# A DRAM to DRAM copy as the first DMA of the ScalarE queue in a pooling kernel

## The chip, the cores and the metric

The kernel runs on one core of a Trainium2 chip. The core has engines that run beside each other: VectorE (DVE), ScalarE (ACT), GpSimd (POOL), SyncE (SP) and TensorE, which has no work here. Data moves between DRAM and the on-chip memory SBUF by 16 DMA engines. A DMA is issued by an instruction on SyncE's or ScalarE's queue; the engine that issued it goes on, and whoever needs the data waits for a semaphore. PSUM is a second, smaller on-chip memory. The metric is device time in microseconds (us) of one execution; lower is better.

## The reference

The input x is 32 x 256 x 4096 float32 (134.2 MB), the output 32 x 256 x 1024 (33.6 MB). Each output is the 2-norm mean over four neighbours:

```python
    for i in range(out_length):
        start = i * kernel_size
        end = start + kernel_size
        window = np.abs(x[:, :, start:end]) ** p
        result[:, :, i] = (np.mean(window, axis=-1)) ** (1.0 / p)
```

with p = 2 and kernel_size = 4, so out = sqrt((a² + b² + c² + d²) / 4).

## The kernel before

All of x is one flat array that is cut into six blocks; each block is laid out as 128 rows, one for each SBUF partition. Blocks 0 to 3 and 4 are cut further into tiles of up to W = 13184 columns: 20 tiles in all, one with 13152 columns (tile 3) and a shorter last one (11680). A tile of W columns is 6592 KB.

Three SBUF buffers `xt` (`X_SLOTS`, tile i in buffer i modulo 3) hold the tiles. `load(i)` (L83) issues tile i's load on SyncE. Its 128 rows are 52,736 bytes each. Three loads are issued at the start (L122-123); load i + 3 is issued when tile i is summed and its buffer is free (L144-145).

For every tile, ScalarE squares it in place (`square`, L89), VectorE adds the two halves of each group of four (`pairs`, L95) and then the two sums that are left (`fours`, L99), and ScalarE takes the root with the factor 1/4 (`root`, L102). The sums of four tiles side by side make one output block in the buffer `ot`; the sum of the first tile of the next block goes to a PSUM buffer `st`, so that it does not wait for the store of `ot`.

There are six stores (`store`, L86). Stores 0, 1 and 2 are issued on ScalarE's queue (L116, called from `roots` for the groups that end in tiles 3, 7 and 11), stores 3, 4 and 5 on SyncE's queue (L147, L168, L172). `rows(flat, b, div)` (L64) gives block b of a flat array as 128 rows; `rows(of, 0, k)` is the part of the output that store 0 writes, 128 rows of 13176 floats, and `rows(xf, 0, 1)` the input of block 0, 128 rows of 52704 floats.

The order of instructions is written out by hand (`manual_schedule`, L62). On ScalarE the first instructions are the load of the function table and a root of one constant column (`first`, L129), which has the table loaded before data arrives. Then follow the squares in tile order, with roots between them. Waits between instructions are put in by the framework from what each one reads and writes; `implied` takes out some that others cover. DMAs take their semaphores from eight, in turn; a DMA that reuses a semaphore waits until the DMA that had it before has landed.

Of the kernel before, what the change touches and what calls it, by code (L numbers as in the profile page):

```python
# [1 line left out]

# [4 lines left out]


@with_exitstack
def kernel(  # L10
    ctx: ExitStack,
    tc: tile.TileContext,
    x: bass.AP,
    p: float,
    kernel_size: int,
    out: bass.AP,
):

    nc = tc.nc

    assert float(p) == 2.0, "kernel specialized for p == 2"
    k = int(kernel_size)  # L30
    assert k == 4, "kernel specialized for kernel_size == 4"

    P = nc.NUM_PARTITIONS
    fp32 = mybir.dt.float32
    Act = mybir.ActivationFunctionType
    add = mybir.AluOpType.add
    xf = x.rearrange("b c l -> (b c l)")
    of = out.rearrange("b c l -> (b c l)")
    total = xf.shape[0] // P

    W = 13184
    R = W // k
    X_SLOTS = 3
    NARROW = W - 32
    LAST = total - 18 * W - NARROW
    widths = [W] * 3 + [NARROW] + [W] * 15 + [LAST]
    n = len(widths)
    assert 0 < LAST <= W and LAST % 16 == 0


    blocks = [[0, 1, 2, 3], [4, 5, 6, 7], [8, 9, 10, 11], [12, 13, 14, 15], [18, 16, 17], [19]]
    block_of = {i: b for b, group in enumerate(blocks) for i in group}
    block_width = [sum(widths[i] for i in group) for group in blocks]

    x_pool = ctx.enter_context(tc.tile_pool(name="x_pool", bufs=1))
    o_pool = ctx.enter_context(tc.tile_pool(name="o_pool", bufs=1))
    s_pool = ctx.enter_context(tc.tile_pool(name="s_pool", bufs=1, space=bass.MemoryType.PSUM))
    x_tiles = [x_pool.tile([P, W], fp32, name=f"xt{j}") for j in range(X_SLOTS)]
    o_tile = o_pool.tile([P, 4 * R], fp32, name="ot")
    first = o_pool.tile([P, 1], fp32, name="first")  # L60
    s_tile = s_pool.tile([P, 4096], fp32, name="st")
    ctx.enter_context(tc.manual_schedule())  # L62

    def rows(flat, b, div):  # L64
        at = sum(block_width[:b]) * P // div
        return flat[at:at + block_width[b] * P // div].rearrange("(p w) -> p w", p=P)


    free = x_tiles[17 % X_SLOTS]
    place = {i: o_tile[:, i % 4 * R:i % 4 * R + widths[i] // k] for i in range(16)}  # L70
    place[18] = free[:, R:2 * R]
    place[19] = free[:, 0:LAST // k]
    place[16] = free[:, 2 * R:3 * R]
    place[17] = free[:, 3 * R:4 * R]
    held = [o_tile[:, 0:w // k] for w in block_width[:4]] + [free[:, R:4 * R], place[19]]

    xs, loads, stores, sums, squares = {}, {}, {}, {}, {}

    def load(i):
        b = block_of[i]  # L80
        at = sum(widths[j] for j in blocks[b][:blocks[b].index(i)])
        xs[i] = x_tiles[i % X_SLOTS][:, 0:widths[i]]
        loads[i] = nc.sync.dma_start(out=xs[i], in_=rows(xf, b, 1)[:, at:at + widths[i]])  # L83

    def store(b, queue):
        stores[b] = queue.dma_start(out=rows(of, b, k), in_=held[b])  # L86

    def square(v):
        return nc.scalar.activation(out=v, in_=v, func=Act.Square)  # L89

    def pairs(v):

        q = v.rearrange("p (n j) -> p n j", j=k)
        h = v[:, 0:v.shape[1] // 2].rearrange("p (n j) -> p n j", j=2)
        return nc.vector.tensor_tensor(out=h, in0=q[:, :, 0:2], in1=q[:, :, 2:4], op=add)  # L95

    def fours(o, v):
        h = v[:, 0:v.shape[1] // 2].rearrange("p (n j) -> p n j", j=2)
        return nc.vector.tensor_tensor(out=o, in0=h[:, :, 0], in1=h[:, :, 1], op=add)  # L99

    def root(o, s):
        return nc.scalar.activation(out=o, in_=s, func=Act.Sqrt, scale=1.0 / k)  # L102

    summed = {i: s_tile[:, 0:R] if i in (4, 8, 12, 16) else place[i] for i in range(n)}

    def roots(*group):
        if len(group) == 1:
            root(place[group[0]], summed[group[0]])
        else:
            v = o_tile[:, group[0] % 4 * R:(group[-1] % 4 + 1) * R]  # L110
            r = root(v, v)
            if group[0] in (5, 9):

                implied(r, stores[block_of[group[0]] - 1])
        if group[-1] in (3, 7, 11):
            store(block_of[group[-1]], nc.scalar)  # L116

    def implied(later, earlier):

        tc.declare_no_dep(later.ins, earlier.ins, reason="implied by the other waits")  # L120

    for i in range(X_SLOTS):  # L122
        load(i)


    ahead = {4: (3,), 8: (7,), 12: (11,)}
    behind = {3: [(0, 1, 2)], 7: [(5, 6), (4,)], 11: [(9, 10), (8,)], 14: [(12,)], 15: [(13, 14)], 16: [(15,)]}

    root(first[:, :], nc.const_aps.tensor(1.0, (P, 1), fp32))  # L129
    for i in range(17):  # L130
        if i in ahead:
            roots(*ahead[i])
        s = square(xs[i])
        squares[i] = s
        if i == 3:
            implied(s, squares[0])
        if i in (3, 7, 11):

            for earlier in sums[i - X_SLOTS]:
                implied(s, earlier)  # L140
        for group in behind.get(i, []):
            roots(*group)
        sums[i] = pairs(xs[i]), fours(summed[i], xs[i])
        if i + X_SLOTS < n:  # L144
            load(i + X_SLOTS)

    store(3, nc.sync)  # L147
    square(xs[17])
    pairs(xs[17])
    fours(summed[17], xs[17])  # L150
    later = {18: 4608, 19: 2000}

    def shared_square(i):
        v = xs[i][:, 0:later[i]]
        nc.vector.tensor_tensor(out=v, in0=v, in1=v, op=mybir.AluOpType.mult)  # L155
        square(xs[i][:, later[i]:widths[i]])

    def shared_pairs(i):
        implied(pairs(xs[i]), loads[i])

    shared_square(18)
    roots(16)
    roots(17)
    shared_pairs(18)
    fours(summed[18], xs[18])
    shared_square(19)
    roots(18)
    store(4, nc.sync)  # L168
    shared_pairs(19)
    fours(summed[19], xs[19])  # L170
    roots(19)
    store(5, nc.sync)  # L172


# [1 line left out]
_INS = ['x', 'p', 'kernel_size']  # L176
_OUTS = [((32, 256, 1024), 'float32')]

_NUMBERS = {'p': 2.0, 'kernel_size': 4}


# [26 lines left out]
```

## Time and profile before

| | |
|---|---|
| median of 3 runs | 393.97 us (393.89 to 394.08) |
| span of the profiled execution | 392.3 us (its only time on the page; 1.7 us under the median) |
| VectorE busy | 218.2 us, 56%, 42 instructions |
| ScalarE busy | 274.4 us, 70%, 37 instructions |
| HBM read, written | 134.22 MB, 33.55 MB, together 428 GB/s over the span |
| chain that ended last | DMA 43%, ACT 30%, DVE 23% |
| a square of a full tile (L89) | 11.19 us |
| `pairs`, `fours` of a full tile (L95, L99) | 7.03, 3.59 us |

The span runs from the first to the last instruction of the profiled execution; the timed runs include what lies around it. In the slices of the page a digit is the busy share in tenths. "To landing" is the time from the issue of a DMA to its last byte's arrival. A group in the profile names the line, the engine, the operation and the tiles; "ACTq" and "SPq" are DMA issues on those queues, which are not counted as busy time. Bracketed at the end of a timeline's line is how long the engine was idle before, and what ended that.

### The profile page before, as it was taken

The page shows a single profiled execution, that of the slowest core. Times are in us where ns is not written, and L with a number is a line of the kernel's source. Part 1 is how long each engine was busy: PE and PEld are TensorE (multiplying, and loading weights), DVE is VectorE, ACT ScalarE, POOL GpSimd, SP SyncE. Part 2 cuts the span into 40 slices and gives each one's busy share as a digit, 9 for nine tenths or more (in the row PEclk, how much of TensorE's full clock was granted, in tenths as well). Part 3 has the DMA queues.
Part 4 walks back from the last instruction along what each step waited for, and adds up shares of the span by engine and source line. Part 5 has one row for each costly group of instructions (what it writes and reads, how often), then busy time and mean ns, then how long its engine had stood idle before and what let it go on. Part 6 is the DMA issues. An engine that isn't in the chain of part 4 may idle for free.

```text
span 392.3 us, 176 instructions
## 1 busy us (share of the span) xinstructions
DVE 218.2 (56%) x42; ACT 274.4 (70%) x37; POOL 0.2 (0%) x4
## 2 busy tenths in 40 slices
DVE  0009477580693274905942748069418485699970
ACT  1095695979950859799509597995098999969910
POOL 0000000000000000000000000000000000000000
DMA  8999999999999999999999999999999999999997
GB/s 344 430 430 430 430 440 435 452 457 366 430 430 430 430 430 430 430 441 446 452 446 441 436 430 436 430 430 430 430 430 430 430 430 430 430 453 415 430 413 342
DMA packets 3744, 167.77 MB, mean 428 GB/s; under 512 B 416, under 2 KB 416, under 8 KB 416
## 3 DMA queue, kind: packets, MB, share of 16 engines
q1 hardware_dynamic: 3312, 147.53, 87.4%
q10 hardware_dynamic: 432, 20.25, 11.9%
HBM read 134.22 MB, written 33.55 MB: 428 GB/s over the span
## 4 chain that ended last, share of the span: by engine, by line
DMA 43%; ACT 30%; DVE 23%; issue 0%; ACTq 0%; SPq 0%; DVEq 0%
DMA xt<-in_x_dram 43%; ACT xt L89 28%; DVE xt L95 14%; DVE ot L99 5%; DVE xt L99 3%; DVE xt L155 2%; ACT ot L102 2%; ACT xt L102 1%; ACTq L86 0%; SPq L83 0%; DVEq L95 0%
## 5 line engine op out<-in xcount | busy, mean ns | idle before, releaser
L89 ACT ACTIVATE xt<-xt 128x13184 f32<-128x13184 f32 (+3 forms) x20 | 216.7, 10847 | 92.3 <-DMA xt<-in_x_dram 91.0
L95 DVE TENSOR_TENSOR xt<-xt 128x6592 f32<-128x6592 f32 (+2 forms) x20 | 139.7, 6985 | 144.1 <-ACT xt L89 143.9
L99 DVE TENSOR_TENSOR ot<-xt 128x3296 f32<-128x3296 f32 (+1 forms) x13 | 46.7, 3592 | 17.9 <-DMA out_dram<-ot 17.6
L102 ACT ACTIVATE ot<-ot 128x6592 f32<-128x6592 f32 (+3 forms) x8 | 37.2, 4655 | 7.0 <-DVE ot L99 7.0
L102 ACT ACTIVATE xt<-xt 128x3296 f32<-128x3296 f32 (+1 forms) x3 | 8.5, 2836 | 8.8 <-DVE xt L99 8.8
L99 DVE TENSOR_TENSOR st<-xt 128x3296 f32<-128x3296 f32 x4 | 14.4, 3600 | 0.1
L99 DVE TENSOR_TENSOR xt<-xt 128x3296 f32<-128x3296 f32 (+1 forms) x3 | 10.4, 3461 | 0.1
L102 ACT ACTIVATE ot<-st 128x3296 f32<-128x3296 f32 x3 | 8.7, 2898 | 0.0
L155 DVE TENSOR_TENSOR xt<-xt 128x4608 f32<-128x4608 f32 (+1 forms) x2 | 7.2, 3593 | 0.0
L102 ACT ACTIVATE xt<-st 128x3296 f32<-128x3296 f32 x1 | 2.9, 2898 | 0.0
L102 ACT ACT_TABLE_LOAD x1 | 1.3, 1283 | 0.7 <-PEq L189 0.7
L102 ACT ACTIVATE first<-const-float32-1.0 128x1 f32<-128x1 f32 x1 | 0.2, 202 | 0.0
L189 POOL MEMSET const-bfloat16-1.0<- 128x1 bf16 x1 | 0.1, 101 | 0.0
L189 POOL MEMSET const-uint8-127<- 128x1 uint8 x1 | 0.1, 101 | 0.0
L189 POOL MEMSET const-float32-0.0<- 128x1 f32 x1 | 0.1, 98 | 0.2 <-issue 0.2
L189 POOL MEMSET const-float32-1.0<- 128x1 f32 x1 | 0.1, 98 | 0.0
## 6 DMA issues: line engine op xcount, KB each, us to landing
xt<-in_x_dram SPq DMA_DIRECT2D x18, 6592.0 KB, 29.8
out_dram<-ot ACTq DMA_DIRECT2D x2, 6592.0 KB, 35.1
out_dram<-ot SPq DMA_DIRECT2D x1, 6592.0 KB, 37.1
out_dram<-ot ACTq DMA_DIRECT2D x1, 6588.0 KB, 36.3
xt<-in_x_dram SPq DMA_DIRECT2D x1, 6576.0 KB, 24.7
xt<-in_x_dram SPq DMA_DIRECT2D x1, 5840.0 KB, 21.9
out_dram<-xt SPq DMA_DIRECT2D x1, 4944.0 KB, 16.1
out_dram<-xt SPq DMA_DIRECT2D x1, 1460.0 KB, 8.2
```

The lines of the kernel that those rows point to most:

```text
L89: return nc.scalar.activation(out=v, in_=v, func=Act.Square)
L95: return nc.vector.tensor_tensor(out=h, in0=q[:, :, 0:2], in1=q[:, :, 2:4], op=add)
L99: return nc.vector.tensor_tensor(out=o, in0=h[:, :, 0], in1=h[:, :, 1], op=add)
L102: return nc.scalar.activation(out=o, in_=s, func=Act.Sqrt, scale=1.0 / k)
L155: nc.vector.tensor_tensor(out=v, in0=v, in1=v, op=mybir.AluOpType.mult)
L189: nc = _bacc.Bacc("TRN2", target_bir_lowering=False, num_devices=1)
```

## The change

After the three first loads have been issued, and ahead of ScalarE's first instruction, ScalarE's queue gets one DMA from DRAM to DRAM. It reads every eighth of the 128 rows of block 0 of x, 2048 floats of each, and writes them to every eighth of the 128 rows that store 0 writes later: 16 rows of 8192 bytes, 131,072 bytes in all. Store 0 overwrites all of them with the result. No other instruction is changed or moved in its queue.

```diff
     for i in range(X_SLOTS):
         load(i)
+    BULK = 2048
+    nc.scalar.dma_start(out=rows(of, 0, k)[0:P:8, 0:BULK], in_=rows(xf, 0, 1)[0:P:8, 0:BULK])
 
 
     ahead = {4: (3,), 8: (7,), 12: (11,)}
```

Since the copy and store 0 write the same bytes, store 0 waits for the copy. The copy takes the first of the eight DMA semaphores, so that the semaphore of every later DMA moves by one; load 6 is now the first to reuse one, the copy's.

## The prediction

> **What bounds the kernel now.** I read the page first, for the DMA row over the 40 slices and for the queues.
>
> ```profile
> DMA  8999999999999999999999999999999999999997
> GB/s 344 430 430 430 430 440 435 452 457 366 430 430 430 430 430 430 430 441 446 452 446 441 436 430 436 430 430 430 430 430 430 430 430 430 430 453 415 430 413 342
> ...
> q1 hardware_dynamic: 3312, 147.53, 87.4%
> q10 hardware_dynamic: 432, 20.25, 11.9%
> ```
>
> The DMA engines are full from the second slice to the last but one, while DVE has 56% and ACT 70% of the span. q1 carries what SyncE issues, q10 what ScalarE issues: the three first stores, 20.25 MB. One slice away from the two ends is low: the tenth, 88 to 98 us, with 366 GB/s at a full DMA row.
>
> Second view, the timeline of ScalarE; each square starts 0.02 us after its load has landed if ScalarE was waiting.
>
> ```profile
> 0.73 1.28 ACT L102 ACT_TABLE_LOAD   x1 [0.73 <-PEq L189]
> 0.73 338.28 SPq L83 DMA_DIRECT2D xt<-in_x_dram  x20
> ...
> 18.79 11.19 ACT L89 ACTIVATE xt<-xt 128x13184 f32<-128x13184 f32 x1 [16.56 <-DMA xt<-in_x_dram]
> ...
> 34.35 11.19 ACT L89 ACTIVATE xt<-xt 128x13184 f32<-128x13184 f32 x1 [4.38 <-DMA xt<-in_x_dram]
> ...
> 65.47 11.16 ACT L89 ACTIVATE xt<-xt 128x13152 f32<-128x13152 f32 x1 [4.34 <-DMA xt<-in_x_dram]
> ...
> 90.31 0.38 ACTq L86 DMA_DIRECT2D out_dram<-ot  x1
> 90.73 22.27 ACT L89 ACTIVATE xt<-xt 128x13184 f32<-128x13184 f32 x2 [0.46 <-ACT ot L102]
> ...
> 128.86 11.19 ACT L89 ACTIVATE xt<-xt 128x13184 f32<-128x13184 f32 x1 [15.86 <-DMA xt<-in_x_dram]
> ```
>
> One load of 6.75 MB takes 34.35 - 18.79 = 15.56 us, 434 GB/s, at full stream. Load 0 was issued at 0.73 and landed at 18.77, 18.04 us later: 2.48 us more than its bytes take, the price of starting from an empty stream.
>
> Third view, windows laid between such landings. Each of the three holds four transfers of the same bytes, three loads and one store of ScalarE's queue (loads 4 to 6 and store 0; loads 8 to 10 and store 1; loads 12 to 14 and store 2). The columns are the window, its length, the busy time of DVE, ACT and POOL with their counts, the clock, the DMA share and GB/s.
>
> ```profile
> 65.47:128.86 63.39, 36.70 (x8) 44.71 (x6) 0.00 (x0) 1.00 1.00 426
> 144.41:206.65 62.24, 36.67 (x8) 44.80 (x7) 0.00 (x0) 1.00 1.00 434
> 222.22:284.49 62.27, 36.81 (x8) 44.80 (x6) 0.00 (x0) 1.00 1.00 434
> ...
> 92.00:96.00 4.00, 0.00 (x0) 4.00 (x1) 0.00 (x0) 1.00 1.12 395
> 96.00:100.00 4.00, 0.00 (x0) 4.00 (x1) 0.00 (x0) 1.00 0.97 422
> ...
> 171.00:175.00 4.00, 0.00 (x0) 4.00 (x1) 0.00 (x0) 1.00 1.03 448
> ```
>
> The first stretch is 63.39 - 62.26 = 1.13 us longer for the same work. The four-microsecond windows place the loss: 92 to 96 us, 1.7 us after store 0 was issued, has 395 GB/s at a share of 1.12; the same place behind store 1 (171 to 175) has 448. In the packet records of the trace every one of the 16 engines has one row of a *load* that starts at 91.9 to 92.4 us and takes 2.6 to 3.1 us; the usual row takes 1.947. The first rows of store 0 start only behind these. So **the first DMA of ScalarE's queue makes all 16 engines stand still for about 1 us; the second and third do not.** SyncE's first store, at 339.10, shows no such loss, though it is the first store of its queue. The first rows of load 0 took 2.0 to 3.0 us too.
>
> Is the end still bound by DMA, so that a microsecond gained at 92 us arrives there? Store 3 was issued at 339.10 and landed 37.1 us later, at 376.2. Store 4, issued at 371.76, landed 16.1 us later, at 387.9; its 5.06 MB at 434 GB/s are 11.7 us: it began where store 3 ended. Store 5 landed at 391.4, 3.5 us after store 4, and its 1.495 MB are 3.45 us. The stream does not run dry up to the last byte.
>
> **The change part by part.** Nothing is removed. Added is one DMA issue on ScalarE, ahead of its table load, of 16 rows of 8192 bytes, and waits that follow from it.
>
> (1) *Issue on ScalarE.* The nearest row is the first ACTq issue, 0.38 us. Table load and first root (1.28 + 0.20) move from 0.73 to about 1.11. Cover: the 16.56 us that ScalarE idles before 18.79. Cost 0; without that cover, 0.38. SyncE's first loads are on another queue and are not moved.
>
> (2) *Waits.* Store 0 now waits for the copy also (both write the first store's rows), and load 6 does (the copy has taken one of the eight DMA semaphores, so each DMA's number moves by one and load 6 reuses the copy's). Both come at 87 to 90 us, over 80 us after the copy; neither waits. A second wait costs a semaphore instruction; three on L86 of SyncE took 17 ns each. On ScalarE that delays square 4, DVE's sums, and so load 7, which comes at 112.6 and has until load 6 has landed at 128.84: 16 us of cover, cost 0. Later pairs on one semaphore are as far apart as before.
>
> (3) *Bytes of the copy.* 131,072 B at 434 GB/s are 0.30 us on 16 engines, 8192 B each. Ahead of the span the trace has 8 KB packets of 0.31 to 0.55 us, one engine each. Lower bound 0: the copy goes in the 2.48 us before load 0 runs at full rate. Upper bound, beside the opening below, 0.55. I take **+0.30**: all three first loads are queued, so every engine that copies delays load rows.
>
> (4) *The opening of ScalarE's queue* moves from 92 us to 1 to 3 us. At 92 us this takes away **-1.13**. At the start it costs between 0 (it passes beside SyncE's own opening, in the 2.48 us in which no row is at full rate anyway) and 1.13 (it comes behind it and stops the first rows again). I take 0: ScalarE and SyncE both issue at 0.73, the engines hold nothing then, and what is lost at an opening is waiting, not bytes. Below zero nothing is possible: SyncE's first issue does not move, and the rows behind it flow no earlier.
>
> Sum: -1.13 + 0.30 + 0 = **-0.83 us** on the span of 392.26, which gives 391.43. The page has one span and no other time of the profiled execution; the median of the three runs, 393.97, is 1.71 us above the span, and I keep that: **393.14**. Nothing gives the 0.83 back: loads arrive earlier by it, and the squares that wait for them (13 waits on loads) start earlier by as much, then DVE, the slots and the next issues. At the end the chain to store 5 starts from load 17 (landed 331.23, ScalarE idle 0.48 before, itself behind load 15), so it moves too.
>
> A rule that speaks against it, from the Trainium skill, "DMA: Bandwidth & Descriptors", section "Anatomy of one DMA": a DMA costs about 2.0 us fixed plus its bytes over 436 GB/s (fitted on another issue path). By that formula the copy is 2.3 us, and if it all counted the sum would be -1.13 + 2.3 = +1.2 us. The trace disagrees that such a fixed part occupies the engines: loads land 15.56 us apart, which is their bytes alone.
>
> **Rivals.**
> A, the forecast: opening moved under SyncE's own, 393.14. For it: the loss appears once, and the first rows of load 0 show the like. Chance 0.62.
> B, openings in a row: the engines open one queue after the other, so the loss moves to 2 us whole. Then -1.13 + 1.13 + 0.30 = +0.30: 394.27. For it: at 92 us the opening stopped rows of a queue already open. Against: at 0.73 there are none. Chance 0.14; with less than half of the opening hidden it is within 0.27 us of the time before.
> C, slower: the loss belongs to the first transfer from SBUF to DRAM, not to the queue. The copy reads DRAM, so the loss stays at 92 us; at the start are the bytes, and where the copy opens its queue at a price, up to 1.13 more: +0.30 to +1.43, 394.3 to 395.4. It decides from the point where the windows still show 63.4 us for the first stretch. For it: the two "firsts" fall together in this trace and cannot be told apart. Against: the stalled rows are loads, before any store row began. Chance 0.16.
> D, the copy holds the engines for its whole start price, 2.48 us from the row of load 0: -1.13 + 2.48 + 0.30 = +1.65, 395.6. Against: the next DMAs land 15.56 us apart. Chance 0.04. (The rule above belongs here.)
> E, the change does not do what it says: the copy is free and opens nothing, 393.97 (0.02), or its rows are not spread and one engine carries all 131 KB at 27.1 GB/s, 4.8 us: -1.13 + 4.8 = +3.7 (0.02).
>
> **How the numbers follow.** This kernel's measurement tells apart some 0.2%, 0.79 us: faster is below 393.18, slower above 394.76. A lies on the edge; with the copy's price between 0 and 0.55 it runs from 392.84 to 393.4, 0.45 of its chance below the edge and 0.17 above. Faster: 0.45. Same: 0.17 of A, 0.12 of B, 0.04 of C, 0.02 of E, 0.35. Slower: 0.12 of C, 0.04 of D, 0.02 of B, 0.02 of E, 0.20. The time is A's, 393.1. The range takes A and B and the lower end of C with 0.3 for the spread of runs: 392.8 to 394.6; A's own range is 392.8 to 393.5.
>
> **What would show it.** The first stretch of three loads and store 0 should have 62.3 us and the tenth slice 430 GB/s or more: then the loss is gone from there. Load 0 should be landed at 19.07 (+0.30); 20.2 is B, 18.77 a free copy, 21.5 D. Later windows should be unchanged. The forecast is wrong if a 63.4 us stretch remains, or if square 0 starts more than 1.1 us late.

## The result and the profile after

The changed kernel takes 394.56 us (median of 21 runs, 394.29 to 394.99), the kernel before 393.99 us beside it (21 runs, 393.83 to 394.18): 0.57 us more, a ratio of 1.0014 with a 95% interval of 1.0008 to 1.002. That is slower, by less than 0.2%, and less than the 0.79 us that the prediction took as the least that can be told apart. The forecast was 393.1, faster.

The page of the changed kernel, DMA row and queues:

```profile
DMA  8999999999999999999999999999999999999997
GB/s 357 430 430 430 430 429 435 424 430 430 430 430 430 430 430 430 430 430 430 451 446 441 446 435 446 430 430 430 430 430 430 430 430 430 430 448 419 430 420 334
...
q1 hardware_dynamic: 3312, 147.53, 87.3%
q10 hardware_dynamic: 464, 20.38, 12.0%
```

q10 has 0.13 MB more, the copy. The tenth slice now shows 430 GB/s, which is what I had named as a sign that the loss is gone. It is not gone; a slice counts each row where it starts, and the rows have moved by 0.4 us against the slices. The next two views are the ones to go by. First the timeline, start and ScalarE:

```profile
0.73 0.61 ACTq L125 DMA_DIRECT2D out_dram<-in_x_dram  x1
1.37 1.28 ACT L102 ACT_TABLE_LOAD   x1 [1.37 <-PEq L191]
...
19.19 11.19 ACT L89 ACTIVATE xt<-xt 128x13184 f32<-128x13184 f32 x1 [16.32 <-DMA xt<-in_x_dram]
...
65.89 11.16 ACT L89 ACTIVATE xt<-xt 128x13152 f32<-128x13152 f32 x1 [4.33 <-DMA xt<-in_x_dram]
...
90.71 0.35 ACTq L86 DMA_DIRECT2D out_dram<-ot  x1
...
128.98 11.19 ACT L89 ACTIVATE xt<-xt 128x13184 f32<-128x13184 f32 x1 [15.60 <-DMA xt<-in_x_dram]
```

Load 0 is 19.19 - 18.79 = 0.40 us late, and ScalarE still idles 16.32 us before it. At 128.98, behind store 0, only 0.12 us of that are left, and at the end of the span 0.3 (392.6 against 392.3). Then the windows between landings, laid as before (window, length, busy of DVE, ACT, POOL, clock, DMA share, GB/s):

```profile
65.89:128.98 63.09, 36.42 (x8) 44.70 (x5) 0.00 (x0) 1.00 1.00 428
144.56:206.82 62.26, 36.40 (x8) 44.80 (x6) 0.00 (x0) 1.00 1.00 434
222.41:284.69 62.28, 36.59 (x8) 44.80 (x7) 0.00 (x0) 1.00 1.00 434
92.00:96.00 4.00, 0.00 (x0) 4.00 (x1) 0.00 (x0) 1.00 1.19 422
```

The first stretch still has 63.09 us where the two others have 62.27. At 92 to 96 us the share is 1.19 at 422 GB/s, where the window ahead of it (88 to 92 us) has 0.98 at the same rate: rows that start there last longer than their bytes need. The packet records of the trace show the same picture as before: each of the 16 engines has one load row that starts at 92.3 to 92.8 us and takes 2.5 to 3.2 us in place of 1.947, and the first rows of store 0 come only then. (The records do not name the engine; a row is put down to the engine whose last row ended where it starts.) **The stop of all engines has stayed at store 0; the copy only added its bytes.** Its issue line:

```profile
out_dram<-in_x_dram ACTq DMA_DIRECT2D x1, 128.0 KB, 8.7
```

It landed 8.7 us after its issue, at 9.42 us. By the records its 16 rows started at 6.2 to 6.8 us, one on each engine and each 0.309 us, behind two load rows that every engine had taken first. The last row ended at 7.14; the other 2.3 us lie between that and the landing.

The stretch goes by the slowest engine. To compare runs I also use the mean over the 16 engines: the time that the rows near the first approach to the store take beyond their bytes at the usual 27.1 GB/s an engine, summed and divided by 16. It is 0.99 us in the kernel before and 0.89 in the changed one. Below, "us an engine" is this figure.

### The profile page after: what moved, and what is told of

Read it like the earlier page. It is cut to its first block, busy times and chain, and to the rows that moved or that the text cites. A ratio compares the mean times of both kernels' runs of the same rounds, so it can differ in the third digit from the quotient of the medians.

```text
span 392.6 us, 178 instructions
## 1 busy us (share of the span) xinstructions
DVE 218.2 (56%) x42; ACT 274.4 (70%) x37; POOL 0.2 (0%) x4
## 4 chain that ended last, share of the span: by engine, by line
DMA 43%; ACT 30%; DVE 23%; issue 0%; ACTq 0%; SPq 0%; DVEq 0%
DMA xt<-in_x_dram 43%; ACT xt L89 28%; DVE xt L95 14%; DVE ot L99 5%; DVE xt L99 3%; DVE xt L157 2%; ACT ot L102 2%; ACT xt L102 1%; ACTq L86 0%; SPq L83 0%; DVEq L95 0%
```

## The experiments

Medians stand beside those of the kernel before on the same chip. Where only one time is given, the kernel ran once.

**e1: store 0 on SyncE's queue, no copy.** Was it ScalarE's queue that stops the engines?

```diff
-            store(block_of[group[-1]], nc.scalar)
+            store(block_of[group[-1]], nc.sync if group[-1] == 3 else nc.scalar)
```

> The kernel before, without the copy, with one edit: store 0 is issued on SyncE's queue; stores 1 and 2 stay on ScalarE's. Theory S (the stop of all 16 engines belongs to the first transfer from SBUF to DRAM, whichever queue): the stretch of loads 4 to 6 and store 0 keeps about 63.4 us, the stretch of loads 8 to 10 and store 1, now ScalarE's first DMA, keeps 62.25; time 394.0. Theory Q (it belongs to the first DMA of ScalarE's queue that touches SBUF): the first stretch falls to 62.3, the second rises to 63.4; time 394.0. If both stretches show 62.3: 392.9; if both show the loss: 395.1.

394.49 us (11 runs) against 394.08, ratio 1.0011 (1.0002 to 1.002). On SyncE's queue store 0 stands behind load 6, so the transfers come in another order and the stretch runs to load 7. Windows of this run:

```profile
65.66:144.64 78.98, 48.67 (x10) 55.79 (x6) 0.00 (x0) 1.00 1.00 427
144.64:207.43 62.79, 30.24 (x6) 44.80 (x6) 0.00 (x0) 1.00 1.00 430
108.00:112.00 4.00, 3.97 (x2) 4.00 (x1) 0.00 (x0) 1.00 0.78 224
```

The first window holds five transfers, which at 62.26 / 4 take 77.83 us: 1.15 us are lost. The last line, 224 GB/s, and the records place it at the last rows of load 6, at 109.4 to 113.1 us, directly ahead of store 0's rows (1.20 us an engine); at 92 us there is none. SyncE's queue had been in use for 90 us. Store 0 was issued at 90.48 us in this run, so the stop goes with its rows and not with its issue. It comes with store 0 on either queue, and the opening of ScalarE's queue is not its cause. The second window lost 0.5 us, at 181 to 185 us, in the middle of store 1. Store 1 is the first DMA of ScalarE's queue here, but its first rows, at 173 to 177 us, ran at their usual time. The median of 11 runs is up by 0.41, about as much. That a smaller loss goes with the queue is therefore not excluded; why it comes stays open.

**e2: an early store from SBUF in place of the copy.** Is it enough that any store has read SBUF?

```diff
+    nc.vector.memset(o_tile[:, 0:256], 0.0)
+    nc.scalar.dma_start(out=rows(of, 0, k)[:, 0:256], in_=o_tile[:, 0:256])
```

> The kernel before with, in place of the copy from DRAM, an early store of the same 131072 bytes from SBUF: VectorE sets 256 columns of ot to zero at the start, and ScalarE's queue stores these as 128 rows of 1024 bytes into store 0's rows, which store 0 overwrites later. Theories S and Q: the stop moves to the start, the first stretch falls from 63.4 to 62.3 us, and load 0 lands at 19.1 (its 0.30 us of bytes) to 20.2 (with the whole stop added): time 393.2 to 394.3. A third theory, P (the stop belongs to what the stream holds at 92 us, whatever came first): the first stretch keeps 63.1 to 63.4, time 394.3 to 394.6, as with the copy.

394.84 us (11 runs) against 394.08, 1.0019 (1.001 to 1.0028). The first stretch kept 63.17 us, 0.91 us an engine. Of my three theories the third (P) had the place right: a small early store on the same queue, from the same tile, does not take the stop along. Its reason, what the stream holds at 92 us, falls with g1 below. The time lies above P's 394.3 to 394.6: in the profiled execution the span is 392.4 us and the time 394.6, 2.2 us apart where the kernel before has 1.7. The other runs with an early memset (f2, g2, g3) show 2.2 too; why was not looked into.

**e3 and e4: the copy at 512 and at 32768 bytes a row.** What does the copy cost?

```diff
-    BULK = 2048
+    BULK = 128      # e3; e4 has 8192
```

> The changed kernel with the copy cut from 16 rows of 8192 to 16 rows of 512 bytes (8192 bytes in all). If the copy costs its bytes, 0.30 us at 8192 bytes a row, the time is 394.0, within 0.1 of the kernel before, and load 0 lands within 0.1 of 18.77. If the copy costs a fixed price for being there (the rest of the 0.57 us by which the medians differ): 394.25 or more. The stop at 92 us stays by theories S and P.

> The changed kernel with the copy at four times its size, 16 rows of 32768 bytes (524288 bytes). By bytes alone, 4 x 0.30 = 1.21 us: 395.2. With a fixed part of 0.27 us besides, as the medians of the change leave it: 395.45. If a copy that writes DRAM costs more than its bytes, above 395.6. First stretch 63.1 to 63.4 us.

e3: 394.14 us (11 runs), +0.06, 1.0003 (0.9994 to 1.0012); first stretch 62.90. e4: 395.25 us (6 runs), +1.17, 1.0029 (1.0017 to 1.004); first stretch 63.45. By bytes +0.02 and +1.21 were due. In e3 load 0 came 0.25 us late, though the copy's bytes are worth 0.02: the landing of load 0 is a poor gauge (below).

**f1: tile 3 at full width.** Is it store 0's odd row length?

```diff
-    NARROW = W - 32
+    NARROW = W
```

> The kernel before with tile 3 at full width (13184 in place of 13152 columns, the last tile 32 columns shorter), so that store 0 has rows of 52736 bytes like stores 1 to 4, in place of 52704. Theory N (the stop belongs to store 0's own shape, rows whose starts are no multiple of 512 bytes; stores 1 and 2, which have no stop, start theirs on such multiples): the stop is gone, the first stretch has 62.3 us, the time is 392.9. Theory W (it belongs to the first long stream of writes, or to writes after a long time without any): first stretch 63.1 to 63.4, time 394.0.

394.09 us (10 runs) against 394.05, 1.0002 (0.9992 to 1.0011); first stretch 63.19, 0.97 us an engine. The row length is not the cause.

**f2: one early full row on each engine, from SBUF.**

```diff
+    nc.vector.memset(o_tile[:, :], 0.0)
+    nc.scalar.dma_start(out=rows(of, 0, k)[0:P:8, :], in_=o_tile[0:P:8, 0:4 * R - 8])
```

> The kernel before with one early store of 16 full rows of 52704 bytes from ot (set to zero by VectorE first) to every eighth of store 0's rows, on ScalarE's queue, some 10 us into the kernel; 843264 bytes, 1.95 us by bytes. Theory L (the stop belongs to the first long rows from SBUF to DRAM; the early stores and copies so far had at most 32768 bytes a row and at most 1024 from SBUF): the stop shows between 10 and 20 us and not at 92; first stretch 62.3, span 392.3 - 1.1 + 1.95 + 1.1 = 394.3. Theory W with a long time without writes, or N: it stays at 92 us, first stretch 63.1 to 63.4, span 394.2.

397.31 us (one run, beside 394.05), span 395.1. Both happened: rows at 17 to 23 us lost 0.75 us an engine, and store 0 still stopped the engines for 1.04; its stretch took 63.41 us. 843 KB of long rows are stopped for and do not prevent the next stop.

**f3: small copies on the way.** Does the path to DRAM fall asleep without writes?

```diff
         squares[i] = s
+        if i in (0, 1, 2):
+            nc.scalar.dma_start(out=rows(of, 0, k)[0:P:8, i * 128:i * 128 + 128], in_=rows(xf, 0, 1)[0:P:8, 0:128])
```

> The kernel before with three small copies from DRAM to DRAM (16 rows of 512 bytes each) on ScalarE's queue behind the squares of tiles 0, 1 and 2, at about 30, 46 and 61 us, so that no more than 30 us pass without a write before store 0. Theory W with a long time without writes (85 us before store 0 in the changed kernel, 46 before store 1): the stop is gone, first stretch 62.3, time 392.9 to 393.1. Theories L and N: first stretch 63.1 to 63.4, time 394.0 to 394.1.

394.25 us (10 runs) against 394.05, 1.0004 (0.9995 to 1.0014); first stretch 63.11, 1.02 us an engine. Writes of 8 KB do not help. They were issued at the start of the three squares, not behind them; the last landed at 58 us, some 33 us ahead of store 0's issue and so a little more than the 30 us that I had planned. The idle time speaks against itself in the kernel before, too: store 3's rows follow load 19 (360.6 us), 78 us behind the end of store 2, without a stop.

**f4: store 0 reads DRAM in place of SBUF.**

```diff
-        stores[b] = queue.dma_start(out=rows(of, b, k), in_=held[b])
+        source = rows(xf, 0, 1)[:, 0:block_width[0] // k] if b == 0 else held[b]
+        stores[b] = queue.dma_start(out=rows(of, b, k), in_=source)
```

> The kernel before with store 0's rows read from x in DRAM in place of ot, in the same shape, place and queue; block 0 of the output is not the reference's. If the stop belongs to reading SBUF (theory L, or any other on the source), the first stretch falls to 62.3 us and the span to 391.2. If it belongs to what is written (N, W), it stays, 63.1 to 63.4 and 392.3.

401.17 us (one run), span 399.4: neither of the two. There is no single stop at 92 us, but rows run late here and there from 92 to 124 us, 1.5 us an engine in sum; the engines drift apart (load 9 and store 1 take 6 us each from the first engine's landing to the last's), and later stretches lose time too. Useful is what came next: store 1, at 171 us, was the first long store from SBUF in this run, and no engine stopped for it. So it is not the first long read of SBUF either.

**g1: no store 0.** Does the stop belong to store 0 or to whoever comes first?

```diff
-            if group[0] in (5, 9):
+            if group[0] == 9:
...
-        if group[-1] in (3, 7, 11):
+        if group[-1] in (7, 11):
```

> The kernel before without store 0 (block 0 of the output is not written). Theory W (the stop belongs to the first large stream of writes): without store 0 there is no stop at 92 us, and store 1, now the first, brings it: four transfers with store 1 take 63.1 to 63.4 us in place of 62.25, span 392.3 - 15.55 = 376.7. Theory Z (it belongs to store 0's place in the program, about 90 us, whatever store 1 finds): no stop anywhere, span 375.6.

381.07 us (one run), span 379.3. Windows of this run:

```profile
92.00:96.00 4.00, 0.00 (x0) 4.00 (x1) 0.00 (x0) 1.00 1.04 448
156.00:160.00 4.00, 0.00 (x0) 4.00 (x1) 0.00 (x0) 1.00 1.20 396
160.00:164.00 4.00, 0.00 (x0) 4.00 (x1) 0.00 (x0) 1.00 0.88 382
...
130.52:193.74 63.22, 33.79 (x8) 44.80 (x6) 0.00 (x0) 1.00 1.01 427
209.33:271.60 62.27, 36.73 (x8) 44.80 (x6) 0.00 (x0) 1.00 1.00 434
```

At 92 us nothing is lost. The four transfers with store 1, now the first store, take 63.22 us, 0.95 more than those with store 2; the records show 1.18 us an engine, at 157 to 162 us, where the window from 156 has a share of 1.20 at 396 GB/s. **The stop moved to the first long store.** The span is 2.6 us above the 376.7 expected, because ahead of this a load came late: ScalarE idled 7.00 us until 130.52. By the records the engines had run empty: each stood 1.3 to 2.6 us without a row before load 7's first rows, at 113.1 to 114.0 us, and these took 2.2 to 2.9 us in place of 1.947, 0.63 us an engine. So first rows out of an empty stream run long on a queue that has been in use for 112 us too.

**g2 and g3: early stores of all 128 rows, full and 8192 bytes long.** How much must be written early?

```diff
+    nc.vector.memset(o_tile[:, :], 0.0)
+    nc.scalar.dma_start(out=rows(of, 0, k), in_=held[0])      # g3: columns 0 to 2047 of both
```

> The kernel before with one early store of store 0's full shape, 128 rows of 52704 bytes, from ot (set to zero first), on ScalarE's queue at about 15 us; store 0 overwrites it. Theory W by amount (0.84 MB written early did not take the stop away from store 0, 6.7 MB written before store 1 did): the stop comes at 15 to 20 us and store 0 has none; span 392.3 + 15.55 = 407.9, and the four transfers with store 0 take 62.3 us. Theory Z: a stop stays with store 0, 63.1 to 63.4 us, and the span is 407.9 or, with a second stop early, 409.

> As the early store of 128 rows, with 8192 bytes of each row (1048576 bytes, 2.42 us by bytes). Theory W by amount: with 1.05 MB still the stop with store 0, 63.1 to 63.4 us, span 394.7 to 395.8. Theory W by rows (8 long rows on each engine are enough, where one was not): 62.3 us, span 393.6 to 394.7.

g2: 421.54 us (one run), span 419.4, 11.5 us more than expected. The engines came apart early (the early store lands over 8.7 us from the first engine to the last, load 1 over 6.6), so its stretches can't be compared: 64.81 us with store 0, 63.97 with store 1. The records have 1.35 us an engine of late rows at 16 to 20 us, and 0.26 ahead of store 0 in place of 0.99. g3: 397.12 us (one run), span 394.9; first stretch 63.06 against 62.27, 0.70 us an engine. 1.05 MB ahead of it do not take the stop away.

**h1, h2 and h3: the change again, twice its size, and at full size.** The price, and whether it is writing that counts.

```diff
     BULK = 2048      # h1; h2 has 4096
...
# h3
+    nc.scalar.dma_start(out=rows(of, 0, k), in_=rows(xf, 0, 1)[:, 0:block_width[0] // k])
```

> The changed kernel once more, beside the kernel before and the copy of twice its size on one chip. If the copy costs its bytes, 0.30 us: median 0.3 above the kernel before's. If it has a fixed part besides, as the first medians leave room for (0.57): 0.5 to 0.6 above. Load 0 lands 0.3 to 0.45 us later than in the kernel before, and the first stretch keeps 63.0 to 63.4 us.

> The changed kernel with the copy at twice its size, 16 rows of 16384 bytes. By bytes 0.61 us above the kernel before; with a fixed part of 0.27 besides, 0.88.

> The changed kernel with the copy at store 0's full shape, 128 rows of 52704 bytes from DRAM to DRAM as ScalarE's first DMA (6.7 MB, 15.55 us by bytes). If the stop belongs to the first large stream of writes into DRAM, wherever it comes from: store 0 has none, its stretch of four transfers takes 62.3 us as in the run with the early full store from SBUF, and the span is 407.9 or more. If it belongs to the first long store that reads SBUF: the stop stays with store 0, 63.1 to 63.4 us.

h1: 394.43 us (11 runs) against 394.08, +0.35, 1.0008 (0.9999 to 1.0017). Its first stretch took 62.70 us, below the 63.0 to 63.4 that I expected, though 0.84 us an engine are late: in the same kernel the stretch differs by 0.39 from one profile to the other. h2: 394.72 (11 runs), +0.64, 1.0018 (1.0009 to 1.0026), first stretch 63.01. Rows of 512, 8192, 16384 and 32768 bytes cost 0.06, 0.35, 0.64 and 1.17 us where bytes alone make 0.02, 0.30, 0.61 and 1.21. The 0.57 of the first 21 runs lies above that line, and 0.30 at the lower end of its interval (0.3 to 0.8 us); a fixed part is not needed, and not excluded for that set. h3: 416.58 us (one run), span 414.8. Its windows:

```profile
83.65:145.91 62.26, 36.74 (x8) 44.71 (x5) 0.00 (x0) 1.00 1.00 432
161.49:225.64 64.15, 34.53 (x7) 44.80 (x6) 0.00 (x0) 1.00 1.00 432
...
112.00:116.00 4.00, 0.00 (x0) 4.00 (x1) 0.00 (x0) 1.00 1.01 435
```

The stretch of loads 4 to 6 and store 0 takes 62.26 us, and 0.17 us an engine are late near store 0's first rows. The full copy reads no SBUF, and it has taken the stop away. (The next stretch, with store 1, took 64.15 us with 0.3 us an engine late over 80 us: the engines drift apart, load 9 takes 6.1 us from the first engine's landing to the last's.) With f4 and g2 this gives the rule as far as it is shown, by one run each: the engines stop for a full store from SBUF when no long stream of writes to DRAM has gone before it; 8 KB to 1.05 MB written before do not take the stop away, 6.7 MB do, from SBUF or from DRAM. That a long stream from DRAM brings the stop itself is not shown: in f4 and h3 its own rows are late here and there, 1.5 us an engine at 92 to 124 us and 1.8 at 4 to 45, without a single stop. Nor is it that store 0's part of the output must have been written once: stores 1 and 2 write fresh rows in the kernel before, without a stop. Where the limit lies, whether it is bytes or time of writing, and what the engines wait for was not tried and stays open. No version here beats the kernel before: f1, f3, e3 and h1 are the same within their intervals, and the one stream that was large enough to take the stop away, 6.7 MB, costs many times its 1 us.

## Why the prediction was wrong

*The bound* was read rightly. The stream of the DMA engines sets the end: 1.21 us of bytes added in the first 8 us (e4) arrive there as 1.17.

*Steps (1) and (2), issue and waits,* cost nothing, as said. The issue took 0.61 us, not 0.38, under a cover of 16.3 us.

*Step (3), the bytes,* was right in size: +0.30, measured 0.35 in h1 and 0.57 in the first set. That the copy would run in the 2.48 us before load 0 is at full rate was the lower bound, and did not happen; its rows came third on each engine.

The rule of the Trainium skill ("DMA: Bandwidth & Descriptors", "Anatomy of one DMA"), 2.0 us fixed and bytes over 436 GB/s, is fitted there on DMAs that GpSimd issues. For the time of this kernel only its second part counts: by that part the copy is estimated at 0.30 us, and the runs of four sizes agree. Something like the fixed part shows in the landing, 2.3 us after the copy's last row ended; store 0 of the kernel before lands 2.3 us behind its last row too. The engines go on with other rows in that time.

*Step (4) failed:* "At 92 us this takes away -1.13". It took away nothing that can be called the stop: the first stretch went from 63.39 to 63.09 us in place of 62.3, and 0.89 us an engine are left of 0.99. The other half of the step, that opening the queue at the start costs 0, is not contradicted: e3, whose copy of 8 KB opens it, is 0.06 us above the kernel before, within its interval. I had read "the first DMA of ScalarE's queue makes all 16 engines stand still" out of a trace in which that DMA was also the first store, the first long read of SBUF by a DMA and the first long write. Rival C said that these firsts can't be told apart and got 0.16; nothing in the trace spoke for the queue more than for the store. The long first rows of load 0, which I took as the like of it, are no sign of a new queue: in g1 load 7's first rows run long after the engines stood empty. The stalled load rows, which I held against C, do not speak against it: in e1 and g1 they are load rows again, on whichever queue, ahead of the store that comes first. Rival C gave the outcome (394.3 to 395.4), its place and its price. Its reason, the first transfer from SBUF, does not hold: in e2 a first small transfer from SBUF goes ahead and the stop stays with store 0, and h3 takes the stop away without one. The stated range, 392.8 to 394.6, holds the 394.56 only because it took in B and the lower end of C; the forecast's own, 392.8 to 393.5, does not. B's 394.27 is near as well, but by luck: it has the stop moved away from store 0.

*The signs I named:* the stretch was a good one, the slice of the page was not, and load 0 (19.07 forecast, 19.17 measured) is a loose one. In h1 load 0 is 0.77 us late:

```profile
19.56 11.19 ACT L89 ACTIVATE xt<-xt 128x13184 f32<-128x13184 f32 x1 [16.70 <-DMA xt<-in_x_dram]
...
128.96 11.19 ACT L89 ACTIVATE xt<-xt 128x13184 f32<-128x13184 f32 x1 [15.21 <-DMA xt<-in_x_dram]
```

At 128.96 it is where the changed kernel is with a load 0 that was 0.37 us earlier. I read this as the slowest engine's loss at the start being partly evened out in the stop; no run was made to show it.

## What to carry to other kernels

When something happens once, list every "first" that falls on it before choosing one: queue, direction, source, destination, size. Moving the first use of a queue forward with a small DMA can be priced beforehand: on a full stream it costs its bytes, and it gains only if the queue is the cause. To find the cause, take the suspect out altogether (g1) or issue it from elsewhere (e1), and see in the trace whether the loss has moved.

## What the runs showed of the hardware that was not expected

- All 16 DMA engines lose 0.7 to 1.2 us each (13 profiles) directly ahead of the first full store from SBUF, whichever queue issues it and with earlier writes of up to 1.05 MB; 0.17 and 0.26 us behind 6.7 MB of earlier writes (h3 and g2).
- Copying 6.7 MB from DRAM to DRAM in place of store 0 cost 7.1 us of span with the same number of bytes moved (f4, one run). Added at the start, such a copy made the span 22.5 us longer where the bytes make 15.55 (h3, one run); a store of the same size from SBUF there made it 27.1 us longer (g2, one run), so that h3's excess can't be put down to the source.
- An engine serves the two queues row by row, not by bytes. In e2 the early store's rows, 1,024 bytes and 8 on each engine, mostly went one by one between load rows of 52,736 bytes, so that its 128 KB took 19.8 us to land; the changed kernel's copy, with one row on each engine, took 8.7.
- The last landing of a DMA that writes DRAM came 2.3 us after its last row had ended (the copy, and stores 0 to 2 of the kernel before); that of load 0 came 0.4 us after.
